# Copying the two banks of a joined matrix product out of PSUM whole, with the addition of their halves made afterwards in SBUF

## The chip, the cores and the metric

The kernel runs on one core of a Trainium2 chip. The metric is device time in microseconds (us), lower is better. The engines of the core that matter here are TensorE (PE in the profile; its weight loads are PEld), VectorE (DVE), ScalarE (ACT), GpSimd (POOL) and SyncE (SP, which issues most of the loads). Each engine works through its own list of instructions strictly in order; semaphores hold an instruction until what it needs is there.

## The reference

Two layers of a macaron encoder block on 512 tokens of width 1024, in float32. Per layer: a SwiGLU feed-forward block, an attention and convolution block, and a second SwiGLU block, with RMS norms between them. The change lies in the feed-forward blocks, of which there are four:

```python
def swiglu(x, w_gate, w_up, w_down):
    return (jax.nn.silu(x @ w_gate) * (x @ w_up)) @ w_down
...
        x = x + 0.5 * swiglu(rms_norm(x, ffn1_norm[l]), ffn1_w_gate[l], ffn1_w_up[l], ffn1_w_down[l])
...
        x = x + 0.5 * swiglu(rms_norm(x, ffn2_norm[l]), ffn2_w_gate[l], ffn2_w_up[l], ffn2_w_down[l])
```

The hidden width is 2816, which is 22 tiles of 128 columns.

## The kernel before

Activations lie with features on the 128 partitions and the 512 tokens along the free axis. Each float32 operand of a product is split into a high part in a 32-bit matmul type and the rest, and a product is the sum of three matmuls: high by high, high by rest, rest by high (`mm3`, L154, L155, L156). An operand of a matmul therefore costs a cast on ACT (L244, L397) and a subtraction on VectorE (L246, or L162 for activations).

A feed-forward block (`ffn_body`) takes its 22 hidden tiles in 11 pairs, in the chunks (0,2), (2,5), (5,8), (8,11). The two pairs of the first chunk are computed plainly. The nine pairs after them go through `pair`, which computes a 2 by 2 block product (blocks: even and odd features by first and second half of the tokens) with seven products where the plain scheme has eight. After the second and the third chunk `down` multiplies the chunk's activations by the down weights, with the same seven products, once for each half of the output rows (g = 0, 1); the last chunk's down products are plain ones (`group`, 512 columns).

In a pair, TensorE runs the seven products in this order: b11, b21, t2, t3, t1, t4, b22. Four of them (b11, t2, t1, b22; `product`) accumulate one after the other in one PSUM bank, bx; ACT copies bx out after each of the first three (L383). Three (b21, t3, t4) are "joined" (`product_joined`): the high part and the rest of the activation lie side by side in one tile `xj`, so that one matmul of 512 columns (L373) makes high by high in the first 256 columns of a bank and high by rest in the last 256, and a second one (L374) adds rest by high to the first half. The sum of a bank's two halves is the product. A joined product takes two banks, one for the gate and one for the up weights: by for b21, and bz for t3 and then t4. Product t4 goes on accumulating in bz on top of t3, so its first matmul may write a bank of bz only when what is needed of t3 has been read out of it.

That read is the place of the change. `parts` yields, for each bank of bz, the columns c, its first half (`main`) and its second half (`rest`). ACT copies the first half into half of a tile d (L425), VectorE adds the second half from PSUM (L426). When t1 is there (copied by ACT into the second row of the tile r2, named e in the profile), one VectorE instruction of 512 columns subtracts it from d (L429). When t4 is there, VectorE combines bz with the first row of r2 (L432 and L433, per bank), ACT applies silu (L436), VectorE multiplies (L437). After b22, ACT and VectorE do the same for the other half (L439, L440). L445 to L452 with L161 and L162 prepare the operands of `down` from these results (only in pairs of the second and third chunk).

VectorE also makes the weight sums of the next pair or of `down` (L408 to L411; L489 to L496 for `down`). In `down`, `times` runs a product into one of three banks px, py, pz, and `add` (L480) adds a bank into x on VectorE; px is accumulated on from one product to the next, so each product into it waits for the `add` of the one before. The quarters of the weights are loaded by SP (L273) into the buffers fr (4 of them) and raw (3); a load is issued when the last reader of its buffer is done. One operand of some products is completed by GpSimd's accumulating DMA (L390) on top of ACT's negated copy (L389).

The order on each engine is not written by hand: the tile framework's scheduler sets it from a simulated timeline, within the limits that `issue_after` gives. Buffers come from pools: 7 banks ps, 5 tiles t of 512 columns (`tmp`), 4 each of the split weights wh and wl.

Of the kernel before, what the change touches and what calls it, by code (L numbers as in the profile page):

```python
# [12 lines left out]
ALU = mybir.AluOpType  # L13
# [4 lines left out]
S = 512  # L18
# [16 lines left out]
HS = S // 2  # L35
# [39 lines left out]
def encoder_kernel(ctx: ExitStack, tc: tile.TileContext, xT, consts, vecs, rgain, wgu1, wd1, wdq1,  # L75
# [11 lines left out]
    def nm(s):  # L87
        uid[0] += 1
        return f"{s}{uid[0]}"

    def slot(dt=FP, w=S):
        return ring.tile([P, w], dt, tag="r", name=nm("r"))

    def tmp(w=S, dt=FP):
        return tmps.tile([P, w], dt, tag="t", name=nm("t"))

    def bank():
        return psum.tile([P, S], FP, tag="ps", name=nm("ps"))
# [4 lines left out]
    V, A, G, T = nc.vector, nc.scalar, nc.gpsimd, nc.tensor  # L103
# [47 lines left out]
    order = {}  # L151
# [7 lines left out]
    def split(src, made=slot):  # L159
        hi, lo = made(FR), made(FR)  # L160
        order["high"] = A.copy(hi, src).ins  # L161
        order["evicted"] = V.tensor_tensor(lo, src, hi.bitcast(FP), ALU.subtract).ins  # L162
        return hi, lo
# [77 lines left out]
    def split_into(q, src, w=WC):  # L241

        hi = wpool.tile([P, WC], FR, tag="wh", name=nm("wh"))
        A.copy(hi[:, :w], src[:, :w])  # L244
        lo = low()
        order["lo"] = V.tensor_tensor(lo[:, :w], src[:, :w], hi[:, :w].bitcast(FP), ALU.subtract).ins  # L246
        return hi, lo
# [5 lines left out]
    def ffn_body(fpool, l, gx, norm, wgu, wd, wdq, gain, done, w0, halved):  # L253
# [12 lines left out]
        def wide(t):  # L266
            return t.rearrange("p (j t) -> p j t", j=2)

        def quarters(w, n, first=False):

            a = quarter(), quarter() if first else late(), quarter(), quarter()
            for q in range(4):
                nc.sync.dma_start(out=a[q][:, :n], in_=w[q])  # L273
            return *a, late()
# [26 lines left out]
        def after(name):  # L301
            return tc.issue_after(order[name]) if name in order else nullcontext()
# [53 lines left out]
        def product(o, w, n, start, stop):  # L356
            with tc.issue_after(order["pe"]):
                for gu in range(2):
                    for k in range(4):
                        hi, lo = X[n][k // 2]  # L360
                        t = slice(k % 2 * HS, (k % 2 + 1) * HS)
                        c = slice(gu * 512 + k * P, gu * 512 + (k + 1) * P)
                        last = mm3(o[:, gu * HS:(gu + 1) * HS], w[0][:, c], w[1][:, c], hi[:, t], lo[:, t],
                                   start and gu == 0 and k == 0, stop and k == 3, True)
            order["pe"] = last

        def product_joined(os, w, n, start):
            with tc.issue_after(order["pe"]):
                for gu, o in enumerate(os):
                    for k in range(4):  # L370
                        both = X[n][k // 2][:, k % 2]
                        c = slice(gu * 512 + k * P, gu * 512 + (k + 1) * P)
                        T.matmul(o, w[0][:, c], both, start=start and k == 0, stop=False, skip_group_check=True)  # L373
                        last = T.matmul(o[:, 0:HS], w[1][:, c], both[:, 0:HS], start=False, stop=k == 3,  # L374
                                        skip_group_check=True).ins
            order["pe"] = last

        def parts(os):

            return [(slice(gu * HS, (gu + 1) * HS), o[:, 0:HS], o[:, HS:S]) for gu, o in enumerate(os)]  # L380

        def copied(o, src):
            A.copy(o, src)  # L383
            return o
# [8 lines left out]
        def summed(w, src, n=WC, lo=None):  # L393

            lo = subtracted(w, src, n) if lo is None else lo
            hi = wpool.tile([P, WC], FR, tag="wh", name=nm("wh"))
            A.copy(hi[:, :n], src[:, :n])  # L397
            return hi, lo

        def pair(p, quartered):  # L400

            a11, a12, a21, a22, s3 = quarters(wgu[l, p], WC, p == CHUNKS[0][1])
            bx, by, bz = bank(), (bank(), bank()), (bank(), bank())
            product(bx, split_into("a11", a11), "b11", True, True)
            a = copied(tmp(), bx)
            product_joined(by, summed(wgu[l, p, 1], a12), "b21", True)
            with after("first"):
                V.tensor_tensor(s3, a11, a21, ALU.add)  # L408
                V.tensor_tensor(a21, a21, a22, ALU.add)  # L409
                V.tensor_tensor(a11, a11, a21, ALU.add)  # L410
                V.tensor_tensor(a12, a12, a11, ALU.add)  # L411
            s = tmp()
            for c, main, rest in parts(by):
                V.tensor_tensor(a[:, c], a[:, c], main, ALU.add)  # L414
                V.tensor_tensor(a[:, c], a[:, c], rest, ALU.add)
                if c.start == 0:
                    A.activation(s[:, 0:HS], a[:, 0:HS], AF.Silu)
            V.tensor_tensor(s[:, 0:HS], s[:, 0:HS], a[:, HS:S], ALU.mult)
            product(bx, split_into("s2", a11), "t2", False, True)
            r2 = wide(fpool.tile([P, WC], FP, tag="e", name=nm("e"), bufs=1))  # L420
            copied(r2[:, 0], bx)
            product_joined(bz, split_into("s3", s3), "t3", True)
            d = tmp()
            for c, main, rest in parts(bz):
                A.copy(d[:, c], main)  # L425
                V.tensor_tensor(d[:, c], d[:, c], rest, ALU.add)  # L426
            product(bx, split_into("s1", a21), "t1", False, True)
            copied(r2[:, 1], bx)
            order["first"] = V.tensor_tensor(r2[:, 1], d, r2[:, 1], ALU.subtract).ins  # L429
            product_joined(bz, summed(wgu[l, p, 3], a22), "t4", False)  # L430
            for c, main, rest in parts(bz):
                V.tensor_tensor(r2[:, 0, c], main, r2[:, 0, c], ALU.subtract)  # L432
                V.tensor_tensor(r2[:, 0, c], rest, r2[:, 0, c], ALU.add)  # L433
            s2 = tmp()
            s2v = s2.rearrange("p (h t) -> p h t", h=2)
            A.activation(s2v, r2[:, :, 0:HS], AF.Silu)  # L436
            V.tensor_tensor(s2v, s2v, r2[:, :, HS:S], ALU.mult)  # L437
            product(bx, split_into("s4", a12), "b22", False, True)
            A.activation(s[:, HS:S], bx[:, 0:HS], AF.Silu)  # L439
            V.tensor_tensor(s[:, HS:S], s[:, HS:S], bx[:, HS:S], ALU.mult)  # L440
            if not quartered:
                return [split(s), split(s2)]
            h0, h1 = slice(0, HS), slice(HS, S)
            b = slot(FR)
            A.copy(b[:, h0], s[:, h0])  # L445
            V.tensor_tensor(b[:, h1], s[:, h0], b[:, h0].bitcast(FP), ALU.subtract)
            b2 = split(s2)
            u, v = fpool.tile([P, S], FP, tag="u", name=nm("u"), bufs=1), tmp()
            V.tensor_tensor(u[:, h0], s[:, h1], s2[:, h1], ALU.subtract)
            order["u0"] = V.tensor_tensor(u[:, h1], u[:, h0], s[:, h0], ALU.subtract).ins  # L450
            V.tensor_tensor(v[:, h0], s[:, h0], s[:, h1], ALU.subtract)
            V.tensor_tensor(v[:, h1], s2[:, h0], u[:, h1], ALU.add)  # L452
            us = split(u)
            order["u"] = order["evicted"]
            vs = split(v)
            order["v"], order["vh"] = order["evicted"], order["high"]
            return [{"b11": (b[:, h0], b[:, h1]), "b21": [w[:, h0] for w in b2], "b22": [w[:, h1] for w in b2],
                     "t3": [w[:, h0] for w in us], "t2": [w[:, h1] for w in us],
                     "t1": [w[:, h0] for w in vs], "t4": [w[:, h1] for w in vs]}]
# [62 lines left out]
        for p0, p1 in CHUNKS:  # L522
# [3 lines left out]
            for p in range(p0, p1):  # L526
# [21 lines left out]
                elif p < CHUNKS[0][1]:  # L548
                    for r in range(2):
                        ws = [load_w(wgu[l, p, 2 * r + q], WC) for q in range(2)]  # L550
                        o = [bank(), bank()]
# [689 lines left out]
```

## Time and profile before

| | |
|---|---|
| three runs, median | 1804.42 us (1803.56 to 1804.89) |
| the profiled execution's own time | 1804.94 us |
| its span, first to last instruction | 1803.1 us |
| mean granted TensorE clock | 0.998 |
| TensorE busy | 1781.6 us, 99% of the span |
| VectorE busy | 1493.0 us, 83% |
| ACT busy | 1091.9 us, 61% |
| GpSimd busy | 420.2 us, 23% |

A row of the timeline gives start, length, engine, line, operation, the tile written and the tiles read, and, in brackets, how long the engine was idle before it and what ended that. Consecutive instructions overlap: one starts before the end of the one before it is recorded, so the time that an instruction takes of its engine is the distance from its start to the next start, which is shorter than its length. L425 and L426 run 72 times, L429 36 times: nine pairs in each of four feed-forward blocks, two banks a pair.

### The profile page before, as it was taken

What the parts mean: (1) busy time and instruction counts of PE and PEld (TensorE: products, weight loads), DVE (VectorE), ACT (ScalarE), POOL (GpSimd) and SP (SyncE); (2) the same over time, 40 slices, a digit from 0 to 9 for tenths busy, and PEclk for the clock granted to TensorE, in tenths of its full rate; (3) what the DMA queues carried; (4) which work ended last, traced back from release to release, by engine and by line L of the source; (5) the groups of instructions that cost most, each with busy time, mean ns of one, the idle gap of its engine ahead of it and who ended that gap; (6) DMA issues with size and microseconds to landing.
All of it is one profiled execution on the core that took longest, in us unless ns stands there. A gap on an engine that the chain in (4) does not pass through costs nothing. (4 is left out here: it accounts for less than half of the span.)

```text
span 1803.1 us, 29267 instructions
## 1 busy us (share of the span) xinstructions
PE 1781.6 (99%) x11334; PEld 1603.1 (89%) x11334; DVE 1493.0 (83%) x2263; ACT 1091.9 (61%) x1721; POOL 420.2 (23%) x343
## 2 busy tenths in 40 slices
PE   9999999999999999999999999999999999999998
PEld 7899999888788899999888999998978788999997
DVE  7898988689956989898779989876998668989884
ACT  5565656457953575756645656554779435656564
POOL 1000010258943000000310000002689410000102
PEclk9999999999999999999999999999999999999999
DMA  5657574325103466665426575743250125575742
GB/s 167 173 127 182 134 174 125 108 88 136 29 24 100 124 167 160 153 159 129 125 63 169 126 191 122 193 110 111 80 151 3 42 83 161 139 183 134 180 119 74
DMA packets 70412, 226.16 MB, mean 125 GB/s; under 512 B 7936, under 2 KB 8320, under 8 KB 70272
## 3 DMA queue, kind: packets, MB, share of 16 engines
q1 hardware_dynamic: 54000, 169.74, 29.7%
q0 software_dynamic: 16128, 54.53, 17.6%
q8 instruction: 89, 1.46, 0.3%
q14 instruction: 51, 0.42, 0.1%
q10 hardware_dynamic: 144, 0.00, 0.0%
HBM read 222.15 MB, written 2.10 MB: 124 GB/s over the span
## 5 line engine op out<-in xcount | busy, mean ns | idle before, releaser
L155 PE MATMUL ps<-r,wh 128*128 128x256 f32 (+1 forms) x2540 | 805.8, 318 | 0.0
L154 PE MATMUL ps<-r,wh 128*128 128x256 f32 (+1 forms) x2540 | 802.9, 320 | 2.3 <-ACT wh L1060 1.5
L156 PE MATMUL ps<-r,wl 128*128 128x256 f32 (+1 forms) x2348 | 750.0, 321 | 1.7 <-DVE wl L246 1.6
L154 PEld LDWEIGHTS ps<-r,wh 128*128 128x128 f32 x2540 | 480.4, 189 | 44.1 <-ACT wh L138 3.7
L155 PEld LDWEIGHTS ps<-r,wh 128*128 128x128 f32 x2540 | 481.4, 190 | 34.2 <-issue 1.4
L156 PEld LDWEIGHTS ps<-r,wl 128*128 128x128 f32 x2348 | 445.0, 190 | 36.7 <-DVE wl L246 3.2
L373 PE MATMUL ps<-xj,wh 128*128 128x512 f32 x864 | 304.8, 392 | 4.6 <-DVE t L426 4.6
L138 ACT CAST wh<-raw 128x1024 fp32r<-128x1024 f32 (+3 forms) x148 | 132.3, 903 | 203.6 <-PE ps L155 100.3
L390 POOL DMA_DIRECT2D ls<-in_wgu x72 | 62.5, 869 | 734.4 <-ACT ls L389 656.5
L244 ACT CAST wh<-fr 128x1024 fp32r<-128x1024 f32 (+1 forms) x160 | 157.8, 986 | 109.7 <-DVE fr L410 51.3
L144 DVE TENSOR_TENSOR wl<-raw,wh 128x1024 fp32r<-128x1024 f32 (+3 forms) x132 | 145.2, 1108 | 84.7 <-ACT wh L138 84.3
L246 DVE TENSOR_TENSOR wl<-fr,wh 128x1024 fp32r<-128x1024 f32 (+1 forms) x160 | 182.1, 1138 | 20.5 <-ACT wh L244 20.5
L373 PEld LDWEIGHTS ps<-xj,wh 128*128 128x128 f32 x864 | 161.3, 188 | 36.3 <-DVE t L426 6.2
L930 POOL TENSOR_TENSOR y<-y,pr 128x511 f32<-128x511 f32 (+14 forms) x120 | 158.1, 1318 | 54.9 <-ACT pr L926 47.5
L374 PE MATMUL ps<-xj,ls 128*128 128x256 f32 x576 | 161.3, 280 | 0.0
L246 DVE TENSOR_TENSOR wl<-raw,wh 128x1024 fp32r<-128x1024 f32 (+1 forms) x100 | 113.4, 1134 | 14.8 <-ACT wh L244 14.4
L244 ACT CAST wh<-raw 128x1024 fp32r<-128x1024 f32 (+1 forms) x100 | 98.1, 981 | 44.7 <-PE ps L155 27.7
L191 POOL TENSOR_TENSOR r<-r,t 128x512 f32<-128x512 f32 x45 | 75.1, 1678 | 175.7 <-ACT t L187 174.9
L374 PEld LDWEIGHTS ps<-xj,ls 128*128 128x128 f32 x576 | 108.3, 188 | 0.2
L389 ACT ACTIVATE ls<-fr 128x1024 fp32r<-128x1024 f32 (+1 forms) x56 | 56.1, 1001 | 85.3 <-PE ps L374 49.5
L926 ACT ACTIVATE pr<-m,vec 128x511 f32<-128x511 f32 (+14 forms) x120 | 85.8, 737 | 12.4 <-POOL y L930 12.4
L922 DVE SCALAR_TENSOR_TENSOR cv<-m,vec,cv 128x511 f32<-128x511 f32 (+14 forms) x120 | 87.8, 732 | 3.6 <-ACT cv L918 2.2
(242 smaller groups left out, 2926.2 us busy)
## 6 DMA issues: line engine op xcount, KB each, us to landing
fr<-in_wgu SPq DMA_DIRECT2D x112, 512.0 KB, 4.2
ls<-in_wgu POOLq DMA_DIRECT2D x72, 512.0 KB, 6.6
raw<-in_wgu SPq DMA_DIRECT2D x62, 512.0 KB, 4.9
fr<-in_wdq SPq DMA_DIRECT2D x48, 384.0 KB, 5.3
ls<-in_wdq POOLq DMA_DIRECT2D x32, 384.0 KB, 4.7
raw<-in_wd SPq DMA_DIRECT2D x32, 384.0 KB, 3.1
raw<-in_wd SPq DMA_DIRECT2D x32, 256.0 KB, 2.7
raw<-in_wcv SPq DMA_DIRECT2D x16, 512.0 KB, 3.6
```

What stands on the lines that cost most here:

```text
L138: order["cast"] = A.copy(hi[:, :w], raw[:, :w]).ins
L144: (G if kind in POOLW.split() else V).tensor_tensor(lo[:, :w], raw[:, :w], hi[:, :w].bitcast(FP), ALU.subtract)
L154: T.matmul(o, lh, rh, start=first, stop=False, skip_group_check=free)
L155: T.matmul(o, lh, rl, start=False, stop=False, skip_group_check=free)
L156: order["mm"] = T.matmul(o, ll, rh, start=False, stop=last, skip_group_check=free).ins
L244: A.copy(hi[:, :w], src[:, :w])
L246: order["lo"] = V.tensor_tensor(lo[:, :w], src[:, :w], hi[:, :w].bitcast(FP), ALU.subtract).ins
L373: T.matmul(o, w[0][:, c], both, start=start and k == 0, stop=False, skip_group_check=True)
L374: last = T.matmul(o[:, 0:HS], w[1][:, c], both[:, 0:HS], start=False, stop=k == 3, skip_group_check=True).ins
L922: V.scalar_tensor_tensor(acc[:, s:], u[c][:, :S - s], tap(k), acc[:, s:], ALU.mult, ALU.add)
L926: A.activation(pr[:, s:], u[c][:, :S - s], AF.Copy, scale=tap(k))
L930: order["conv"] = G.tensor_tensor(acc[:, s:], acc[:, s:], pr[:, s:], ALU.add).ins
```

## The change

The change is in `pair` alone. ACT now copies each bank of bz whole, 512 columns, into a tile of its own (L383 by way of `copied`); two tiles t stand where one stood. VectorE adds the second half of each tile to its first half in SBUF (now L425). The subtraction of t1 (L429), one instruction of 512 columns over both banks before, is two of 256 columns, one for each tile.

```diff
             product_joined(bz, split_into("s3", s3), "t3", True)
-            d = tmp()
-            for c, main, rest in parts(bz):
-                A.copy(d[:, c], main)
-                V.tensor_tensor(d[:, c], d[:, c], rest, ALU.add)
+            d = [copied(tmp(), o) for o in bz]
+            for t in d:
+                V.tensor_tensor(t[:, 0:HS], t[:, 0:HS], t[:, HS:S], ALU.add)
             product(bx, split_into("s1", a21), "t1", False, True)
             copied(r2[:, 1], bx)
-            order["first"] = V.tensor_tensor(r2[:, 1], d, r2[:, 1], ALU.subtract).ins
+            for t, (c, _, _) in zip(d, parts(bz)):
+                order["first"] = V.tensor_tensor(r2[:, 1, c], t[:, 0:HS], r2[:, 1, c], ALU.subtract).ins
             product_joined(bz, summed(wgu[l, p, 3], a22), "t4", False)
```

The scheduler was run anew, and it moved some instructions. The lists of GpSimd and SP have the same order as before. Where the lists of the other three engines differ is shown at three places.

First, TensorE and ACT in the third pair of the second chunk. The rows of TensorE are the end of t1 (L154 to L156, into bx) and the start of t4 (L373 and L374, into the first bank of bz); what an instruction waits for stands in brackets. Before:

```order
L156 MATMUL ps_1213<-r_670,wl_1337 128x256
L154 MATMUL ps_1213<-r_670,wh_1335 128x256
L155 MATMUL ps_1213<-r_671,wh_1335 128x256
L156 MATMUL ps_1213<-r_670,wl_1337 128x256
L373 MATMUL ps_1216<-xj_507,wh_1368 128x512 [waits DVE_49]
```

And now:

```order
L156 MATMUL ps_1217<-r_670,wl_1342 128x256
L154 MATMUL ps_1217<-r_670,wh_1340 128x256
L155 MATMUL ps_1217<-r_671,wh_1340 128x256
L156 MATMUL ps_1217<-r_670,wl_1342 128x256
L373 MATMUL ps_1220<-xj_507,wh_1374 128x512 [waits Activation_49]
```

The order is the same; t4's first matmul waits for an instruction of ACT where it waited for one of VectorE.

ACT's rows there, from the copies of bz (t) to the silu of b22 (L439), before:

```order
L425 COPY t_1330<-ps_1216 128x256
L425 COPY t_1330<-ps_1217 128x256 [waits PE_49]
L397 COPY wh_1482<-raw_1445 128x768 [waits PE_49]
L383 COPY e_1308<-ps_1213 128x512 [waits PE_49]
L445 COPY r_1423<-t_1273 128x256 [waits DVE_49]
L389 ACTIVATE ls_1530<-fr_1447 128x768 [waits DMAHW5_49,DMASW5_49,PE_49]
L244 COPY wh_1506<-fr_1444 128x768 [waits DVE_49,Activation_49]
L436 ACTIVATE t_1390<-e_1308 128x512 [waits DVE_49,Activation_49]
L244 COPY wh_1533<-raw_1452 128x768 [waits PE_49]
L439 ACTIVATE t_1273<-ps_1213 128x256 [waits PE_49]
```

And now:

```order
L383 COPY t_1334<-ps_1220 128x512
L383 COPY t_1336<-ps_1221 128x512 [waits PE_49]
L397 COPY wh_1488<-raw_1451 128x768 [waits PE_49]
L383 COPY e_1312<-ps_1217 128x512 [waits PE_49]
L445 COPY r_1429<-t_1277 128x256 [waits DVE_49]
L389 ACTIVATE ls_1536<-fr_1453 128x768 [waits DMAHW5_49,DMASW5_49,PE_49]
L436 ACTIVATE t_1396<-e_1312 128x512 [waits DVE_49,Activation_49]
L439 ACTIVATE t_1277<-ps_1217 128x256 [waits PE_49]
L244 COPY wh_1512<-fr_1450 128x768 [waits DVE_49]
L244 COPY wh_1539<-raw_1458 128x768
```

The two copies are whole banks, and the two casts L244 for `down` stand behind the two silus L436 and L439 instead of between and before them.

Second, VectorE at the end of the same pair, from the last L433 (t4 taken into r2) to the first `add` of `down` (L480). Before:

```order
L433 TENSOR_TENSOR e_1308<-ps_1217,e_1308 128x256
L246 TENSOR_TENSOR wl_1508<-fr_1444,wh_1506 128x768
L437 TENSOR_TENSOR t_1390<-t_1390,e_1308 128x512
L440 TENSOR_TENSOR t_1273<-t_1273,ps_1213 128x256
L449 TENSOR_TENSOR u_1430<-t_1273,t_1390 128x256
L162 TENSOR_TENSOR r_1427<-t_1390,r_1426 128x512
L451 TENSOR_TENSOR t_1431<-t_1273 128x256
L450 TENSOR_TENSOR u_1430<-u_1430,t_1273 128x256
L480 TENSOR_SCALAR x<-ps_1453,x 128x2x256
```

And now:

```order
L433 TENSOR_TENSOR e_1312<-ps_1221,e_1312 128x256
L440 TENSOR_TENSOR t_1277<-t_1277,ps_1217 128x256
L437 TENSOR_TENSOR t_1396<-t_1396,e_1312 128x512
L451 TENSOR_TENSOR t_1437<-t_1277 128x256
L246 TENSOR_TENSOR wl_1514<-fr_1450,wh_1512 128x768
L449 TENSOR_TENSOR u_1436<-t_1277,t_1396 128x256
L162 TENSOR_TENSOR r_1433<-t_1396,r_1432 128x512
L450 TENSOR_TENSOR u_1436<-u_1436,t_1277 128x256
L480 TENSOR_SCALAR x<-ps_1459,x 128x2x256
```

L440, which needs b22, now stands ahead of L437 and of the weight subtraction L246; the same eight instructions follow the last L433 up to L480.

Third, TensorE in the last pair of the last chunk, where the scheduler had put eight matmuls of a plain down product (L154 to L156 with 512 columns) between the two banks of t4. Before:

```order
L374 MATMUL ps_3346<-xj_696,ls_3495 128x256
L154 MATMUL ps_3561<-r_3099,wh_3564 128x512 [waits Activation_49]
L155 MATMUL ps_3561<-r_3100,wh_3564 128x512
L156 MATMUL ps_3561<-r_3099,wl_3566 128x512 [waits DVE_49]
L154 MATMUL ps_3561<-r_3103,wh_3564 128x512
L155 MATMUL ps_3561<-r_3104,wh_3564 128x512
L156 MATMUL ps_3561<-r_3103,wl_3566 128x512
L154 MATMUL ps_3561<-r_3326,wh_3564 128x512
L155 MATMUL ps_3561<-r_3327,wh_3564 128x512
L373 MATMUL ps_3347<-xj_507,wh_3498 128x512 [waits DVE_49]
L374 MATMUL ps_3347<-xj_507,ls_3495 128x256
```

And now:

```order
L374 MATMUL ps_3362<-xj_696,ls_3513 128x256
L373 MATMUL ps_3363<-xj_507,wh_3516 128x512 [waits Activation_49]
L374 MATMUL ps_3363<-xj_507,ls_3513 128x256
L373 MATMUL ps_3363<-xj_507,wh_3516 128x512
L374 MATMUL ps_3363<-xj_507,ls_3513 128x256
L373 MATMUL ps_3363<-xj_696,wh_3516 128x512
L374 MATMUL ps_3363<-xj_696,ls_3513 128x256
L373 MATMUL ps_3363<-xj_696,wh_3516 128x512
L374 MATMUL ps_3363<-xj_696,ls_3513 128x256
L154 MATMUL ps_3579<-r_3113,wh_3582 128x512 [waits PE_49]
L155 MATMUL ps_3579<-r_3114,wh_3582 128x512
```

The second bank of t4 follows the first at once, and the eight matmuls come after it. This happens once in each feed-forward block.

## The prediction

> **What bounds the kernel now.** I read the page first, for which engine is full:
>
> ```profile
> PE 1781.6 (99%) x11334; PEld 1603.1 (89%) x11334; DVE 1493.0 (83%) x2263; ACT 1091.9 (61%) x1721; POOL 420.2 (23%) x343
> ```
>
> TensorE is busy 99% of the span, and the change takes no matmul away. It can gain only what TensorE waits. So the list of waits comes next (who waited for whom: us in total, times, longest); the last row is VectorE's largest wait for TensorE.
>
> ```profile
> PE ps L373 <- DVE t L426: 4.6, 8, 0.6
> PE ps L156 <- DVE wl L246: 1.6, 6, 0.3
> DVE e L432 <- PE ps L374: 40.5, 28, 1.7
> ```
>
> The first row is the wait that the change is about: the first matmul of t4 waits until VectorE has read bz in L426. It happens 8 times in 36 pairs: two in each feed-forward block, in the third pairs of the second and the third chunk. The chain of work that ended last passes through it (start, length, what):
>
> ```profile
> 1662.67 0.34 DVE t L426
> 1663.06 0.50 PE ps L373
> ```
>
> The timeline of TensorE shows the first of the eight; idle counts only from the modelled end of a matmul, so the starts tell more.
>
> ```profile
> 128.97 0.28 PE L156 MATMUL ps<-r,wl 128*128 128x256 f32 x1
> 129.82 0.50 PE L373 MATMUL ps<-xj,wh 128*128 128x512 f32 x1 [0.57 <-DVE t L426]
> 130.15 0.28 PE L374 MATMUL ps<-xj,ls 128*128 128x256 f32 x1
> 130.27 0.39 PE L373 MATMUL ps<-xj,wh 128*128 128x512 f32 x1
> ```
>
> A 256-column matmul starts 0.12 us after the one before (130.15 to 130.27), so L373 could have started at 129.09: it is 0.73 late. It is also 0.50 long where the next L373 has 0.39: a restart costs 0.10 more. Each wait costs **0.84 us**, and all eight 6.7 us, if nothing else becomes late. That is the question of this prediction.
>
> **The cost of each part.** These groups (count, busy us, mean ns) price the copies and additions:
>
> ```profile
> L425 ACT COPY t<-ps 128x256 f32<-128x256 f32 x72 | 25.5, 366 | 0.0
> L383 ACT COPY t<-ps 128x512 f32<-128x512 f32 x36 | 20.9, 579 | 0.0
> L426 DVE TENSOR_TENSOR t<-t,ps 128x256 f32<-128x256 f32 x72 | 29.1, 412 | 0.0
> L418 DVE TENSOR_TENSOR t<-t,t 128x256 f32<-128x256 f32 x36 | 15.1, 419 | 5.9 <-ACT t L417 5.9
> ```
>
> A whole-bank copy takes ACT 579 - 366 = 213 ns more: 72 of them 15.4 us. An addition with both inputs in SBUF is L418: 419 against 412 ns, which is no difference (72 times 7 ns is 0.5 us). Splitting L429 puts two 256-column starts where one of 512 columns was; by the distances of starts below (0.335 and 0.60 us) that is 0.07 us a pair, 2.5 us in all. I cost ACT's and VectorE's extra time at nothing because both idle in each pair for another reason. ACT is idle 1.14 us right behind the two copies at the critical place, until TensorE frees a buffer for L397:
>
> ```profile
> 127.40 0.63 ACT L425 COPY t<-ps 128x256 f32<-128x256 f32 x2
> 129.17 0.83 ACT L397 CAST wh<-raw 128x768 fp32r<-128x768 f32 x1 [1.14 <-PE ps L155]
> 136.38 0.38 ACT L439 ACTIVATE t<-ps 128x256 f32<-128x256 f32 x1
> 140.04 0.85 ACT L389 ACTIVATE ls<-raw 128x768 fp32r<-128x768 f32 x1 [0.44 <-PE ps L156]
> 142.03 0.83 ACT L397 CAST wh<-fr 128x768 fp32r<-128x768 f32 x1
> ```
>
> VectorE's cover is the 40.5 us at L432 above. Without these covers the price is 0.43 us a pair on ACT and 0.07 on VectorE.
>
> The removed wait: the two copies end at 127.40 + 0.63 + 2 x 0.213 = 128.5 at the latest, and t4 now waits for them instead of L426, which began at 129.36. 128.5 is ahead of 129.09, so **the wait goes entirely**, and what was behind L426 on VectorE no longer counts for t4. The eight matmuls that change places with the second bank of t4 in the last chunk I cost at nothing: that wait is not in the list of waits at this place, and the work is the same.
>
> Here the Trainium skill, VectorE: DVE Perf Modes, section "Rules for kernel authors", speaks against the change: it says to read a matmul's output straight from PSUM unless many operations follow the copy, and here one follows. By it the copies buy nothing and the sum would be 0 us. The trace agrees that the addition gets no faster (412, 419 ns), but the rule doesn't count who waits for the bank, and the 0.73 us at 129.82 does.
>
> **What is late next.** VectorE, behind the place, in the pair's end and the start of `down`:
>
> ```profile
> 134.96 0.95 DVE L246 TENSOR_TENSOR wl<-fr,wh 128x768 fp32r<-128x768 f32 x1
> 135.82 0.68 DVE L437 TENSOR_TENSOR t<-t,e 128x512 f32<-128x512 f32 x1
> 136.79 0.42 DVE L440 TENSOR_TENSOR t<-t,ps 128x256 f32<-128x256 f32 x1 [0.28 <-ACT t L439]
> 137.59 0.68 DVE L162 TENSOR_TENSOR r<-t,r 128x512 fp32r<-128x512 f32 x1
> 138.19 0.42 DVE L451 TENSOR_TENSOR t<-t 128x256 f32<-128x256 f32 x1
> 138.86 0.68 DVE L480 SCALAR_TENSOR_TENSOR x<-ps,x 128x512 f32<-128x512 f32 x1
> ...
> 143.33 0.68 DVE L480 SCALAR_TENSOR_TENSOR x<-ps,x 128x512 f32<-128x512 f32 x1
> ...
> 148.22 0.96 DVE L489 TENSOR_TENSOR raw<-fr,fr 128x768 f32<-128x768 f32 x1 [0.79 <-DMA fr<-in_wdq]
> ...
> 154.54 0.95 DVE L246 TENSOR_TENSOR wl<-fr,wh 128x768 fp32r<-128x768 f32 x1
> ```
>
> And TensorE, at the end of b22 and where `down` needs VectorE:
>
> ```profile
> 135.43 0.28 PE L156 MATMUL ps<-xs,wl 128*128 128x256 f32 x1
> ...
> 139.84 0.28 PE L154 MATMUL ps<-r,wh 128*128 128x256 f32 x1
> ...
> 144.16 0.36 PE L154 MATMUL ps<-r,wh 128*128 128x256 f32 x1
> ...
> 155.10 0.28 PE L155 MATMUL ps<-r,wh 128*128 128x256 f32 x1
> 155.55 0.39 PE L156 MATMUL ps<-r,wl 128*128 128x256 f32 x1 [0.16 <-DVE wl L246]
> 155.77 0.28 PE L154 MATMUL ps<-r,wh 128*128 128x256 f32 x1
> ```
>
> 1. b22 ends 0.84 earlier, at 135.43 + 0.28 - 0.84 = 134.87. In the new order no cast stands ahead of L439, so it runs at 134.91 to 135.29, and L440 starts at 135.33.
> 2. From L440 to the first L480 the new order has L440, L437, L451, L246, L449, L162, L450: four of 256 columns at 0.335 (138.19 to 138.86 is two), two of 512 at 0.60 (137.59 to 138.19), one of 768 at 0.86 (134.96 to 135.82): 3.40 us. L480 starts at 138.73 instead of 138.86: **0.1 us earlier, not 0.84**, since L437 and L246 ran before the wait for L439 and now run behind it.
> 3. The matmul at 139.84 accumulates in px and needs this L480, which ended at 139.54. The nearest that one such pair comes is 144.16 - (143.33 + 0.68) = 0.15, where the matmul is already held (0.36 long against 0.28). So it may start at 139.54 - 0.1 + 0.15 = 139.59; it would come at 139.00, and is held. The matmul at 144.16 is at its limit already and moves with its L480, 0.1. **Of 0.84 us, 0.1 is left at 144.16.**
> 4. At 155.55 TensorE waits again, for L246. The start is 0.45 behind 155.10 and the next 0.22 behind that, against 0.12 each: 0.43 us lost for an idle of 0.16. VectorE's chain to it starts with a wait for a load at 148.22. That load goes out here:
>
> ```profile
> 142.89 0.88 SPq L273 DMA_DIRECT2D fr<-in_wdq  x2
> ```
>
> It follows ACT's L397 (142.03 + 0.83), two instructions behind L389 at 140.04, which waited for TensorE. TensorE reaches that point 0.84 earlier (it lies ahead of 139.84), and then L389 is held only by the cast behind L450, done at about 139.4. So L389, L397, the load and VectorE from 148.22 on come **0.6 us earlier** (VectorE itself is free 0.1 earlier, and had idled 0.79 there). L246 then ends before TensorE asks, and the 0.43 us go.
>
> **The sum.** Eight places keep 0.1: 0.8 us. The list shows six waits for L246, 1.6 us of idle; each loses 0.43 - 0.16 = 0.27 more than its idle: 1.6 + 6 x 0.27 = 3.2 us. Together **4.0 us**; at each of the six places that is 0.1 + 0.53, about what VectorE moves (0.6). The profiled execution took 1804.94, 1.8 more than its span, and that part doesn't change; less 4.0 it is 1800.9. The median of the runs is 0.52 lower, so the forecast is **1800.4 us**. About 0.2%, 3.6 us, is what a measurement of this kernel can tell from no change; the forecast lies only just beyond it.
>
> **The rivals.** *Given back whole.* If the load at 142.89 comes no earlier, or lands no earlier, VectorE reaches 154.54 as before, TensorE waits there longer, and only 0.1 a place is left: 0.8 us, 1803.6. For it: the 0.79 us that VectorE waits for this load. Against it: its issue hangs on ACT, which waited for TensorE. Chance 0.28; half gains, up to 3.6 us, belong here.
>
> *All kept.* If the L480s come earlier than I make them, the direct 6.7 us stay, and with the 3.2 behind them 9.9: 1794.5; with either alone short, about 1797.5. For it: eight clean waits. Against it: step 2, whose terms are all rows. Chance 0.11.
>
> *Slower.* ACT's whole copies push its later work. The sharpest place is the copy of b11 out of bx in the second and third pair of each chunk, 24 places:
>
> ```profile
> 119.69 0.58 ACT L383 COPY t<-ps 128x512 f32<-128x512 f32 x1
> ...
> 120.53 0.28 PE L154 MATMUL ps<-r,wh 128*128 128x256 f32 x1
> ```
>
> The copy ends 0.26 before the matmul that writes its bank; 0.15 is the distance at which one is held, so a delay over 0.11 us shows. VectorE's 0.07 stays under it. If ACT's 0.43 arrived there, 24 x 0.32 = 7.7 us would be lost against 4.0 gained: 1808.1. Against it: the 1.14 us of idle on ACT swallow it in the same pair. The rule of the Trainium skill named above points this way. Chance 0.06. That the change doesn't do what it says I can exclude: the first matmul of t4 now waits for ACT.
>
> **How the numbers follow.** The forecast has 0.55, with its own range 1799.4 to 1802: 0.44 of it beyond 3.6 us, 0.11 within. So faster 0.44 + 0.11 = 0.55; same 0.11 + 0.28 = 0.39; slower 0.06. The range runs from part of "all kept" (1797.5) to past "given back" (1804.2), and leaves the slower case out.
>
> **What would show it.** No wait of L373 for L425 in the list. At each of the eight places TensorE gains 0.84, is held at the second accumulation into px (139.84 here) for about 0.6, and passes the point of 155.55 without a wait, 0.5 us earlier. The load of 142.89 is issued 0.6 earlier. VectorE has 36 instructions more and some 3 us more of busy time, ACT 15 us more. The forecast is wrong if the waits for L246 in `down` grow (given back), if the first L480 moves by much more than 0.1 (all kept), or if TensorE starts to wait for L383 (slower).

## The result, and the profile after

The changed kernel takes **1798.88 us** (median of 10 runs, 1798.58 to 1800.76) against 1803.98 us for the kernel before (median of 10, 1802.33 to 1806.11). The ratio is 0.9973, with a 95% interval of 0.9963 to 0.9983: 5.1 us faster, between 3.1 and 6.7. The whole interval lies on the faster side, though its near end, 0.17%, is just short of the 0.2% that the prediction takes a measurement to tell. The time is inside the predicted range; the forecast was 1800.4. The span of the profiled execution went from 1803.1 to 1797.1 us.

The page of the changed kernel has the same matmuls, 36 VectorE instructions more for 1.5 us more of VectorE time, and 15.6 us more of ACT:

```profile
PE 1781.8 (99%) x11334; PEld 1602.4 (89%) x11334; DVE 1494.5 (83%) x2299; ACT 1107.5 (62%) x1721; POOL 421.5 (23%) x343
```

The list of TensorE's waits begins with this row. Both waits that the prediction speaks of, for the reader of t3's bank (4.6 us, 8 times) and for L246 (1.6 us, 6 times), are gone from it:

```profile
PE ps L834 <- ACT r L840: 2.7, 6, 0.7
```

The timeline of TensorE at the first of the eight places (start, length):

```profile
128.90 0.28 PE L156 MATMUL ps<-r,wl 128*128 128x256 f32 x1
129.01 0.40 PE L373 MATMUL ps<-xj,wh 128*128 128x512 f32 x1
...
134.52 0.28 PE L156 MATMUL ps<-xs,wl 128*128 128x256 f32 x1
...
138.22 0.28 PE L154 MATMUL ps<-r,wh 128*128 128x256 f32 x1
138.47 0.38 PE L155 MATMUL ps<-r,wh 128*128 128x256 f32 x1
...
139.04 0.28 PE L156 MATMUL ps<-r,ls 128*128 128x256 f32 x1
139.41 0.39 PE L154 MATMUL ps<-r,wh 128*128 128x256 f32 x1
...
143.98 0.36 PE L154 MATMUL ps<-r,wh 128*128 128x256 f32 x1
...
154.91 0.29 PE L155 MATMUL ps<-r,wh 128*128 128x256 f32 x1
155.04 0.28 PE L156 MATMUL ps<-r,wl 128*128 128x256 f32 x1
155.16 0.28 PE L154 MATMUL ps<-r,wh 128*128 128x256 f32 x1
```

Read it beside the rows of before, matmul by matmul, as the lead of the changed kernel. Ahead of the place the lead is 128.97 - 128.90 = 0.07 us. At t4's first matmul it is 129.82 - 129.01 = 0.81, and that matmul has no restart (0.40 long, not 0.50); at the end of b22 0.91. At the second product into px (t2) it is 139.84 - 139.41 = 0.43, at the third (t1) 144.16 - 143.98 = 0.18, at 155.10 still 0.19, and behind the wait for L246 155.77 - 155.16 = 0.61. So of the 0.84 us gained at the wait 0.11 is left at t1, and 0.43 comes back at L246.

The same reading at all eight places, from the row ahead of t4 to the one that answers to 155.77, gives 0.54, 0.73, 0.51, 0.59, 0.86, 0.75, 0.63 and 0.11 us: **4.7 us**. The last place had no wait for L246 to lose: there the load landed in time in the kernel before too (the row's two loads took 4.5 us, shown at e3 and e5).

The two profiled executions differ by 6.0 us, not 4.7. One stretch that the change does not touch, about 1402 us into the kernel before, adds 1.5 us, and 0.25 us is lost about 456 us into it. The next two fences show the stretch for before and after, by windows (stretch, its length, TensorE's busy time and instructions, granted clock, share of the DMA engines, GB/s):

```profile
1400.00:1403.00 3.00, 2.68 (x7) 0.65 0.00 0
```

```profile
1396.00:1399.00 3.00, 2.33 (x10) 1.00 0.00 0
```

The granted clock was 0.65 there in the one execution and 1.00 in the other. The matmuls of 512 columns show it, before and after:

```profile
1403.27 0.63 PE L155 MATMUL ps<-m,wh 128*128 128x512 f32 x1
1403.70 0.63 PE L156 MATMUL ps<-m,wl 128*128 128x512 f32 x1
```

```profile
1398.52 0.39 PE L155 MATMUL ps<-m,wh 128*128 128x512 f32 x1
1398.75 0.39 PE L156 MATMUL ps<-m,wl 128*128 128x512 f32 x1
```

They start 0.43 us apart in the one and 0.23 in the other, and the lead grows by 1.5 us in this stretch. The Trainium skill, TensorE: Matmul & The Clock Gate, section "What's actually happening", says that the clock has two states, half and full; 0.43 against 0.23 us agrees with that. The profiled executions of four of the twelve runs below (e5, e7, e11, e12) met the low clock there too; all four contain the change, so the change does not remove it. The medians do not hang on it: the executions with a mean granted clock of 1.0 have a median of 1803.7 us before (15 of them, from the series of the experiments) and 1798.9 us after (6), a difference of 4.8.

VectorE at the place and behind it, in the changed kernel:

```profile
135.26 0.42 DVE L440 TENSOR_TENSOR t<-t,ps 128x256 f32<-128x256 f32 x1 [0.48 <-ACT t L439]
135.59 0.68 DVE L437 TENSOR_TENSOR t<-t,e 128x512 f32<-128x512 f32 x1
...
136.53 0.95 DVE L246 TENSOR_TENSOR wl<-fr,wh 128x768 fp32r<-128x768 f32 x1
...
137.74 0.68 DVE L162 TENSOR_TENSOR r<-t,r 128x512 fp32r<-128x512 f32 x1
...
138.67 0.68 DVE L480 SCALAR_TENSOR_TENSOR x<-ps,x 128x512 f32<-128x512 f32 x1
...
147.16 0.95 DVE L489 TENSOR_TENSOR raw<-fr,fr 128x768 f32<-128x768 f32 x1
```

L489 no longer waits for its load and starts 1.06 us earlier than in the kernel before (148.22). ACT and SP there:

```profile
129.10 0.83 ACT L397 CAST wh<-raw 128x768 fp32r<-128x768 f32 x1 [0.71 <-PE ps L155]
134.84 0.38 ACT L439 ACTIVATE t<-ps 128x256 f32<-128x256 f32 x1 [0.87 <-PE ps L156]
139.36 0.85 ACT L389 ACTIVATE ls<-raw 128x768 fp32r<-128x768 f32 x1
141.36 0.83 ACT L397 CAST wh<-fr 128x768 fp32r<-128x768 f32 x1
```

```profile
142.22 1.37 SPq L273 DMA_DIRECT2D fr<-in_wdq  x2
```

ACT's idle time behind the two copies fell from 1.14 to 0.71 us, by the 0.43 of the wider copies, and the load goes out 0.67 us earlier.

### The profile page after: what moved, and what is told of

The parts are those of the page before. It is cut to its first block, busy times and chain, and to the rows that moved or that the text cites. A ratio compares the mean times of both kernels' runs of the same rounds, so it can differ in the third digit from the quotient of the medians.

```text
span 1797.1 us, 29235 instructions
## 1 busy us (share of the span) xinstructions
PE 1781.8 (99%) x11334; PEld 1602.4 (89%) x11334; DVE 1494.5 (83%) x2299; ACT 1107.5 (62%) x1721; POOL 421.5 (23%) x343
## 4 chain that ended last, share of the span: by engine, by line
PE 91%; ACT 3%; DVE 2%; POOL 2%; issue 1%; DMA 0%; SPq 0%; ACTq 0%; POOLq 0%; DVEq 0%
PE ps L154 24%; PE ps L156 23%; PE ps L155 23%; PE ps L373 11%; PE ps L374 6%; PE ps L868 1%; PE ps L834 1%; POOL y L930 1%; ACT pr L926 1%; ACT r L840 1%; PE ps L855 1%; PE ps L198 0%; POOL sck L173 0%; PE ps L217 0%; DVE wl L246 0%
## 5 line engine op out<-in xcount | busy, mean ns | idle before, releaser
L154 PE MATMUL ps<-r,wh 128*128 128x256 f32 (+1 forms) x2540 | 803.6, 320 | 2.2 <-ACT wh L138 0.7
L156 PE MATMUL ps<-r,wl 128*128 128x256 f32 (+1 forms) x2348 | 749.2, 321 | 0.0
L154 PEld LDWEIGHTS ps<-r,wh 128*128 128x128 f32 x2540 | 480.5, 189 | 47.0 <-ACT wh L138 3.6
L156 PEld LDWEIGHTS ps<-r,wl 128*128 128x128 f32 x2348 | 445.1, 190 | 33.5 <-DVE wl L144 0.4
L373 PE MATMUL ps<-xj,wh 128*128 128x512 f32 x864 | 303.9, 392 | 0.0
L390 POOL DMA_DIRECT2D ls<-in_wgu x72 | 62.7, 871 | 734.7 <-ACT ls L389 595.3
L244 ACT CAST wh<-fr 128x1024 fp32r<-128x1024 f32 (+1 forms) x160 | 157.6, 985 | 104.4 <-DVE fr L410 53.2
L246 DVE TENSOR_TENSOR wl<-fr,wh 128x1024 fp32r<-128x1024 f32 (+1 forms) x160 | 182.3, 1139 | 20.3 <-ACT wh L244 20.3
L373 PEld LDWEIGHTS ps<-xj,wh 128*128 128x128 f32 x864 | 161.4, 188 | 30.1
L374 PE MATMUL ps<-xj,ls 128*128 128x256 f32 x576 | 161.3, 280 | 0.0
L244 ACT CAST wh<-raw 128x1024 fp32r<-128x1024 f32 (+1 forms) x100 | 98.2, 982 | 45.1 <-PE ps L155 24.2
L246 DVE TENSOR_TENSOR wl<-raw,wh 128x1024 fp32r<-128x1024 f32 (+1 forms) x100 | 113.5, 1135 | 14.2 <-ACT wh L244 13.7
L374 PEld LDWEIGHTS ps<-xj,ls 128*128 128x128 f32 x576 | 108.3, 188 | 0.0
L389 ACT ACTIVATE ls<-fr 128x1024 fp32r<-128x1024 f32 (+1 forms) x56 | 56.1, 1002 | 74.5 <-PE ps L374 42.8
```

The lines of the kernel that those rows point to most:

```text
L154: T.matmul(o, lh, rh, start=first, stop=False, skip_group_check=free)
L156: order["mm"] = T.matmul(o, ll, rh, start=False, stop=last, skip_group_check=free).ins
```

## The experiments

The theory at the start: the lasting gain is made at the eight places alone, 0.1 us each directly and 0.4 to 0.6 behind it, where the load of L273 lands earlier and L246 is no longer late. Each time stands beside runs of the kernel before on the same chip, in the same series.

**e1 and e2: the places alone, and all the others.** In e1 only the third pairs (p = 4 and 7) have the change, in e2 only the other pairs:

```diff
+            whole = p in (4, 7)          # e2: p not in (4, 7)
+            if whole:
+                d = [copied(tmp(), o) for o in bz]
...
+            else:
+                d = tmp()
...
```

> The kernel before with the change made only in the third pair of chunks 2 and 3, that is at 8 of the 36 places. Theory (the gain is the wait for L373 at these 8 places and what follows from it): about the whole gain of the change, 4 to 5 us off the kernel before, ratio near 0.9974, and no row of TensorE waiting for L373's bank in the profile. Rival (the gain is spread over all 36 pairs, or comes from the order of the last chunk): 8/36 of it, about 1 us, ratio near 0.9994.

> The kernel before with the change in the 28 pairs other than those of the third-pair places. Theory: the 8 waits for L373 stay at 0.73 us each and the time is that of before within 0.5 us, ratio 0.9997 to 1.0003. Rival (the gain is spread over all pairs, or comes from the order of the last chunk): 28/36 of it or more, about 4 us, ratio near 0.998.

e1: 1799.08 us against 1803.68, ratio 0.9974 (0.9964 to 0.9984). e2: 1804.52 us, ratio 1.0005 (0.9997 to 1.0014). The list of e2 still has both waits:

```profile
PE ps L373 <- DVE t L432: 5.8, 8, 1.3
...
PE ps L156 <- DVE wl L246: 1.3, 5, 0.3
```

The whole gain comes from 8 of the 36 pairs. The other 28, with the new order of the last chunk and 11 us more of ACT (1103.0 against 1091.9), change nothing that can be measured.

**e4: twice the copies.** Each bank of bz is copied twice by ACT:

```diff
-            d = [copied(tmp(), o) for o in bz]
+            d = [copied(copied(tmp(), o), o) for o in bz]
```

> The changed kernel, in which ACT copies each bank of the fourth product twice: 72 more copies of 0.53 us, about 38 us more of ACT's time and 1.06 us more at each place, five times what the change added to ACT. Theory (ACT has idle time that hides this: 1.14 us at the place before the change, 0.71 us after it): mostly hidden, within 0.2% of the changed kernel, though the place's cast L397 comes up to 0.35 us later. Rival (ACT's copies are on the path, so the change already pays for its 15 us of ACT with part of its gain): slower than the changed kernel by several us, 72 x 0.2 us = 15 us if the extra copy's price is like that of the wider one.

1799.20 us against 1803.68, ratio 0.9977 (0.9967 to 0.9987): as fast as the changed kernel within what can be told, with 34.8 us more of ACT than that (1142.3 against 1107.5). ACT at the place:

```profile
127.07 2.03 ACT L383 COPY t<-ps 128x512 f32<-128x512 f32 x4
128.97 0.86 ACT L397 CAST wh<-raw 128x768 fp32r<-128x768 f32 x1
```

The four copies fill the idle time wholly: L397 follows without a gap. t4's first matmul is not held even so. The cover on ACT was real, and larger than the change needs.

**e6: only the earlier load, without the change.** In the kernel before, the high cast of the fourth weight quarter (L397) is made together with its L389:

```diff
-                lo = subtracted(wdq[l, g, chunk, 3], a22, n)
+                both = summed(wdq[l, g, chunk, 3], a22, n)
...
-                    times(pz, a22, "t4", False, 3, lo)
+                    times(pz, a22, "t4", False, 3, both)
```

> The kernel before, without the change, in which ACT's cast L397 of the fourth weight quarter stands together with L389 of the same quarter, ahead of the casts of the third product, so that the DMA of L273 goes out earlier. Theory: the wait for L373 stays (8 places, 0.73 us), the wait for L246 goes at about 7 places: 3 us faster than the kernel before, ratio 0.998 to 0.9987. Rival (the wait for L246 hangs on the change itself, through VectorE's order or TensorE's earlier start): no faster than the kernel before, ratio 0.9997 to 1.0003, with the wait for L246 still in the list.

1799.85 us against 1804.21, ratio 0.9975 (0.9965 to 0.9985). SP's row has the first of the two loads now at 136.16, the second still at 136.16 + 7.27 - 0.33 = 143.10:

```profile
136.16 7.27 SPq L273 DMA_DIRECT2D fr<-in_wdq  x2
```

VectorE's L489 (now L492) starts without a wait, and of TensorE's two waits one is left:

```profile
146.99 0.95 DVE L492 TENSOR_TENSOR raw<-fr,fr 128x768 f32<-128x768 f32 x1
```

```profile
PE ps L373 <- DVE t L426: 4.6, 8, 0.6
```

So the load alone is worth 4.4 us by the medians (4.0 us by the starts at the eight places), with all eight waits for L373 in place. At t1, counted from the row ahead of t4, TensorE stands within 0.06 us of the kernel before at all eight places, so an earlier start of TensorE is not what removes the wait for L246. **Most of what the change gains can be had without it.** e8 makes both edits:

> The changed kernel with the earlier cast L397 of the run on the kernel before. Theory (with the change the load already lands before VectorE asks for it): within 1 us of the changed kernel, ratio 0.997 to 0.9978; the place where the wait for L246 is left over may gain another 0.4 us. Rival (the load is still late for VectorE at places): 2 us or more faster than the changed kernel, ratio 0.9962 or below.

1798.55 us, ratio 0.9968 (0.9956 to 0.9981), and 4.7 us by the starts at the places, as in the changed kernel. The two gains are one and the same, apart from the 0.1 us of a place.

**e3 and e5: the load issued later again.** In the changed kernel ACT makes the cast L397, which sets the buffer free, once more (e3) or three times more (e5):

```diff
+                    if g == 0 and q == 3:
+                        for _ in range(3):          # e3: once
+                            A.copy(hi[:, :n], src[:, :n])
```

> The changed kernel, in which ACT makes the cast L397 of the fourth weight quarter twice in the first column group of the down product, so that the buffer it reads comes free about 0.75 us later and the DMA of L273 is issued about 0.75 us later. Nothing else is touched. Theory (the part of the gain that lasts is the later wait for L246, which went because this DMA is issued earlier): the DMA is issued near 142.9 as in the kernel before, VectorE waits for it again ahead of L489, and the wait of TensorE for L246 returns at 7 of 8 places with 0.4 to 0.65 us: 3 to 4.5 us slower than the changed kernel, ratio to the kernel before 0.999 to 1.000. Rival (that wait went for another reason, VectorE's order or the earlier start of TensorE): as fast as the changed kernel, ratio near 0.9973.

> As the late load of the run before, with three more casts in place of one, so that the DMA of L273 is issued some 2.3 us later than in the changed kernel (about 144.5 on its clock). ACT's 2.62 us idle behind the place holds them. Theory (TensorE's wait for L246 went because VectorE's L489 finds its load landed and starts 1.06 us earlier than before; one extra cast moved L489 by 0 to 0.5 us only, since the load then landed sooner after its issue): L489 now starts as late as in the kernel before or later, the wait for L246 is back at most of the 8 places, and the time is 3 us or more above the changed kernel, 1802 us or more, ratio 0.999 or above. Rival (that wait went for another reason): VectorE starts L489 late and TensorE doesn't wait for L246, 1799 to 1800 us, ratio 0.9975.

e3: 1799.57 us against 1803.68, ratio 0.9977 (0.9968 to 0.9986). e5: 1799.37 us against 1804.21, ratio 0.9972 (0.9962 to 0.9982). Neither is slower than the changed kernel beyond what can be told. Both missed what my theory expected, and the rows tell why. e3's execution lies 1.5 us behind from its first microseconds on, so I count from GpSimd's load L390, which goes out shortly before. Here are that load, SP's row and L489 (L491, L492 in these kernels) of e3:

```profile
142.08 0.86 POOL L390 DMA_DIRECT2D ls<-in_wdq  x1 [6.52 <-ACT ls L389]
...
144.67 0.81 SPq L273 DMA_DIRECT2D fr<-in_wdq  x2
...
148.70 0.95 DVE L491 TENSOR_TENSOR raw<-fr,fr 128x768 f32<-128x768 f32 x1
```

and of e5:

```profile
140.82 0.86 POOL L390 DMA_DIRECT2D ls<-in_wdq  x1 [6.52 <-ACT ls L389]
...
143.57 1.79 SPq L273 DMA_DIRECT2D fr<-in_wdq  x2
...
147.44 0.95 DVE L492 TENSOR_TENSOR raw<-fr,fr 128x768 f32<-128x768 f32 x1
```

The load goes out 2.59 and 2.75 us behind L390, where the changed kernel has 142.22 - 140.50 = 1.72 (row below). Yet L489 starts 6.62 us behind L390 in both, and 147.16 - 140.50 = 6.66 in the changed kernel. The load had landed all the same, for it took less time. The view of the DMA issues gives the size and the median time from issue to landing of the two loads in the row, for before, after, e3 and e5 in this order:

```profile
fr<-in_wdq SPq DMA_DIRECT2D x2, 384.0 KB, 5.5
```

```profile
fr<-in_wdq SPq DMA_DIRECT2D x2, 384.0 KB, 4.5
```

```profile
fr<-in_wdq SPq DMA_DIRECT2D x2, 384.0 KB, 3.9
```

```profile
fr<-in_wdq SPq DMA_DIRECT2D x2, 384.0 KB, 3.5
```

The load that L489 waits for is the first of the two. Over all eight places its own time has the medians 5.3, 4.5, 4.1 and 3.3 us, in the same order. And the load of L390 in the kernel before and in the changed one:

```profile
141.18 0.86 POOL L390 DMA_DIRECT2D ls<-in_wdq  x1 [6.28 <-ACT ls L389]
```

```profile
140.50 0.86 POOL L390 DMA_DIRECT2D ls<-in_wdq  x1 [6.51 <-ACT ls L389]
```

Three loads of 384 KB follow each other: GpSimd's L390, SP's first, SP's second (the end of SP's row less one issue of 0.33). From the first to the third it is 2.3 us in the kernel before (143.44 - 141.18) and 2.8 in the changed one (143.26 - 140.50), about 3 in e3 and 4.2 in e5. In this order the load took less and less time. That the distances are the cause is not shown, though. At the last place of the kernel before the three issues stand as at the other seven, and the two loads took 4.5 us; at the sixth place of e11 (below) they stand as in the changed kernel, and the two took 6.5:

```profile
fr<-in_wdq SPq DMA_DIRECT2D x2, 384.0 KB, 4.5
```

```profile
fr<-in_wdq SPq DMA_DIRECT2D x2, 384.0 KB, 6.5
```

In the changed kernel L390 and SP's first load come 0.68 and 0.67 us earlier, but the second only 0.18, since it waits for VectorE's L246 and not for ACT. So the first load gains twice, by its issue and by a shorter landing. L390 stands as far ahead of it as before (1.72 against 1.71 us), so that distance does not explain the shorter landing; the second load stands 1.04 us behind the first instead of 0.55. Whether that is the reason stays open.

That the landing decides about the wait for L246 can be seen where it came late. In e1, whose issues stand as in the changed kernel, L489 (L499 there) waits for the load at the second place, and that place keeps 0.40 instead of 0.73 us. At the sixth place of e11, VectorE waits for its late load (L504 there), TensorE waits for L246 again, and the place ends 0.45 us behind the kernel before. Here are that row of e1, and the two of e11:

```profile
237.97 0.96 DVE L499 TENSOR_TENSOR raw<-fr,fr 128x768 f32<-128x768 f32 x1 [0.69 <-DMA fr<-in_wdq]
```

```profile
1128.63 0.96 DVE L504 TENSOR_TENSOR raw<-fr,fr 128x768 f32<-128x768 f32 x1 [1.56 <-DMA fr<-in_wdq]
...
1135.97 0.39 PE L156 MATMUL ps<-r,wl 128*128 128x256 f32 x1 [0.30 <-DVE wl L246]
```

**e7: the first L480 earlier.** At the eight places L437 goes ahead of the wait for L439, and L451, L452 and the split of v go behind the first `add`:

```diff
+            with tc.issue_after(order["s2"]) if p in (4, 7) else nullcontext():
+                V.tensor_tensor(s[:, HS:S], s[:, HS:S], bx[:, HS:S], ALU.mult)
...
-                    add(0, 0, px, 1)
+                    order["x0"] = add(0, 0, px, 1)
+                for item in act:
+                    if "rest" in item:
+                        with after("x0"):
+                            item.pop("rest")()
```

> The changed kernel, in which at the 8 places VectorE runs L437 ahead of the wait for ACT's L439, and L451, L452 with the split that hangs on them behind the first L480 of the down product, so that this L480 starts about 0.5 us earlier. Theory (0.74 of the 0.84 us are lost again because this L480 comes only 0.1 to 0.2 us earlier, and TensorE waits for it): TensorE is held less at the second accumulation into px, and each place keeps up to 0.84 us where it keeps 0.55 now: 1.5 to 4 us faster than the changed kernel, 1795 to 1797.5 us, ratio 0.9955 to 0.9966. Rival (TensorE is held there by something else, the weights or the casts of the activation): as fast as the changed kernel, ratio near 0.9973.

1797.43 us against 1804.21, ratio 0.9963 (0.9950 to 0.9975). Later the same kernel ran beside the changed kernel itself:

> The changed kernel itself, so that the next three stand beside it on one chip. All theories: 1798 to 1800 us, ratio 0.9963 to 0.9983 to the kernel before.

> The run with the first L480 earlier once more, beside the changed kernel on one chip. Theory: its profile kept 0.28 us where the changed kernel keeps 0.11 us, at 7 places of 8: 1.2 to 1.4 us faster than the changed kernel, ratio near 0.9963. Rival: no difference, its 1797.4 us was scatter between chips.

e9: 1798.90 us against 1804.49, ratio 0.9968 (0.9956 to 0.9979). e12: 1798.08 us, ratio 0.9964 (0.9950 to 0.9977). The medians put e7's order 0.8 us ahead of the changed kernel side by side (e12 against e9, where 1.2 to 1.4 were expected), and 1.5 us across the series (e7 against the first measurement). The intervals overlap, so the times alone do not prove it. The traces do show the step. VectorE's first `add` (L488 here) and the matmuls that are held, in e7:

```profile
138.22 0.68 DVE L488 SCALAR_TENSOR_TENSOR x<-ps,x 128x512 f32<-128x512 f32 x1
```

```profile
138.96 0.38 PE L154 MATMUL ps<-r,wh 128*128 128x256 f32 x1
...
141.69 0.39 PE L156 MATMUL ps<-r,wl 128*128 128x256 f32 x1
...
143.85 0.36 PE L154 MATMUL ps<-r,wh 128*128 128x256 f32 x1
```

The first `add` is at 138.22 instead of 138.67, and t2's product into px passes 0.45 earlier (138.96 against 139.41), with all of its 0.84 us. But TensorE is now held at 141.69, in the third product's weights (L246), and again at t1. What is left at t1 is 0.28 us instead of 0.11 (0.14 and 0.21 at two places), and the eight places sum to 5.9 us in both profiles instead of 4.7. Between L440 and the `add` ahead of t1, VectorE has hardly a gap; moving work about there gains only the idle time it saves.

**e10 and e11: one row of VectorE's work taken off.** GpSimd stands idle at the place and gets L451:

```diff
-            V.tensor_tensor(v[:, h0], s[:, h0], s[:, h1], ALU.subtract)
+            (G if p in (4, 7) else V).tensor_tensor(v[:, h0], s[:, h0], s[:, h1], ALU.subtract)
```

> The changed kernel, in which the subtraction L451 (128x256, 0.33 us from start to start on VectorE) of the 8 places is made by GpSimd, which stands idle there for 6.5 us. Theory (from the wait for L439 to the L480 at 143.15 VectorE runs without a gap, so what a place keeps of its 0.84 us at the third accumulation into px is what this row of VectorE work gains, 0.11 us now): each place keeps 0.33 us more, 2.6 us in all, 1796 to 1797.5 us, ratio 0.9955 to 0.9963. Rival (ACT's casts or the weights hold TensorE there, or GpSimd's work slows VectorE's): as fast as the changed kernel, within 1 us.

> Both edits: VectorE's order of the run with the first L480 earlier, and L451 on GpSimd. Theory: 0.28 us kept by the order and 0.33 us by the row taken off, up to 0.61 us of the 0.84 us at each of the 8 places: 3.5 to 4 us faster than the changed kernel, 1794.5 to 1796 us, ratio 0.9945 to 0.9957. Rival (another engine holds TensorE once VectorE is earlier): no faster than the run with the order alone, 1797 us.

e10: 1800.55 us against 1804.49, ratio 0.9980 (0.9971 to 0.9989). e11: 1799.49 us, ratio 0.9974 (0.9965 to 0.9984). Both missed what the theory expected: they lie 1.65 and 1.4 us above the runs without this edit (e9 and e12, in the same series). The intervals overlap, but the starts agree: the eight places keep 3.0 us in both, where they keep 4.7 and 5.9 without it (in e11 late loads have a part in that). The cause is the one that e10's rival names last, GpSimd's work slowing VectorE's, and it cost more than the 1 us that the rival allowed. Here is VectorE in e10, and GpSimd beside it:

```profile
135.39 1.50 DVE L246 TENSOR_TENSOR wl<-fr,wh 128x768 fp32r<-128x768 f32 x1
```

```profile
134.96 1.11 POOL L451 TENSOR_TENSOR t<-t 128x256 f32<-128x256 f32 x1 [1.76 <-DVE t L440]
```

L246 takes 1.50 us where the same row takes 0.95: 0.55 lost against 0.33 saved. The place then keeps less than nothing at t1 (-0.10 us). In e11 it is L450, 0.96 against 0.42 us, beside a GpSimd row of 1.55. The Trainium skill, SBUF — State Buffer, section "SBUF: two separate sides", says that VectorE and GpSimd share a pair of ports, which a VectorE instruction with two SBUF inputs and a GpSimd instruction that reads SBUF hold against each other; the 0.55 us here agree with that.

## Why the prediction was right, and where its sizes were off

1. **The wait goes entirely: right.** t4's first matmul starts 0.11 us behind the one before it and has no restart. e1 and e2 put the whole gain at the eight places.
2. **The covers: right.** ACT's idle time shrank by exactly the 0.43 us that the copies cost. e4 shows that twice as many copies cost nothing that can be told, so the rival "slower" was ruled out with room to spare. VectorE's 36 instructions cost nothing (the 28 of them in e2), and its busy time grew by 1.5 us, half of the 3 foreseen.
3. **Steps 1 and 2: right to 0.01 us.** L439, L440 and L480 were forecast at 134.91, 135.33 and 138.73 and stand at 134.84, 135.26 and 138.67; the whole trace is 0.07 ahead there.
4. **Step 3: right in size, with one hold more than foreseen.** TensorE is stopped first at 138.47, for the split L162 of the activation that ends at 138.42, and then at 139.41 for L480. Together 0.5 us are given back (0.91 to 0.43), 0.6 by the forecast: the matmul starts 0.06 us behind the end of L480 (139.35), not 0.15. At t1, where the distance is 0.14, 0.11 us is left, 0.1 by the forecast.
5. **Step 4: the right wait goes, for half of the right reason.** The load was forecast 0.6 us earlier and went out 0.67 earlier, 0.60 without the 0.07 by which the trace is ahead, and the 0.43 us at 155.55 went. But VectorE reaches L489 1.06 us earlier, not 0.6: the time from issue to landing, which the step took as fixed, fell from 5.5 to 4.5 us. Had it stayed, the 0.6 us would have covered most of the wait all the same: by the starts L246 would have come 0.03, 0.15 and 0.04 us late at three places, with a restart of 0.1 at each, 0.5 us in all (an estimate). e3 and e5 show that the issue of this load alone does not decide it. e6 shows that its landing does: with the first load moved alone the wait goes too, and in e1 and e11 it comes back where the load lands late.
6. **The sum: too small.** I gave L246's 3.2 us to six places, those of the list; there are seven, since the view leaves out an idle time this short at one of them (0.14 us). The seven gave 3.9 us: 0.4 came from the seventh, and the rest from longer waits than the first place's. With 0.8 us kept directly, as forecast, the eight places give 4.7 us by the starts instead of 4.0. The medians differ by 5.1, with an interval of 3.1 to 6.7, which holds both.

"Given back whole" failed at its condition: the load did land earlier. "All kept" failed at step 2, as argued. e7 moves the first `add` and keeps more at once, and then shows the next thing that is late, L246 at 141.69. The rule of the Trainium skill weighed in the prediction, read there as a sum of 0 us, does not give the time here, 5.1 us less. The addition got no faster (412 ns from PSUM, 418 ns from SBUF after), and yet the earlier free bank paid, at the eight places where TensorE waited for it.

## What to carry to other kernels

A wait that heads the list can be worth little: its 0.84 us shrank to 0.11 within 15 us, at an engine that works without a gap, and what lasted came from a load whose issue hung on the same chain. So follow each gained interval to the next two or three things that TensorE needs, and test the last link alone: e6 got nearly the whole gain by moving one cast. And time a load by its landing, not by its issue: this load, issued in the same way, took 4.3 to 5.5 us at the eight places of the kernel before.

## What the runs showed of the hardware that was not expected

The load of 384 KB that L489 needs took 4.3 to 5.5 us from issue to landing at the eight places of the kernel before, and 4.3 to 5.0 at those of the changed one; in e11, issued as in the changed kernel, up to 6.5; and in e8, where no other load was issued within 3.5 us of it, 2.9 to 3.2. A GpSimd subtraction of 128x256 made a VectorE instruction of 0.95 us last 1.50. And one stretch of the attention and convolution block ran at a granted clock of 0.65 in some executions and 1.00 in others, 1.5 us apart, behind nearly the same waits of TensorE (0.79 and 0.31 us before, 0.78 and 0.36 after).

The version that beats both kernels is e7's by its medians (1797.43 and 1798.08 us, ratios 0.9963 and 0.9964 to the kernel before). That it beats the changed kernel by 1 us is what its traces show at the eight places, 5.9 against 4.7 us; its times do not show it yet.
